# Window attention: queries and keys projected with their features on partitions, and rotated by a shuffle within 32 partitions

## The chip, the cores and the metric

The kernel runs on one core of one Trainium2 chip. Its time is the device time of one execution in microseconds (us); of three executions the median is given. A profile of one further execution shows what each engine did: TensorE (PE, and PEld for its weight loads), VectorE (DVE), ScalarE (ACT), GpSimd (POOL) and SyncE (SP, which here only issues transfers).

## The reference

An encoder of two layers works on 1024 tokens of 1024 features, all in float32. Layer 0 is the one that matters here: windowed attention with 16 query heads and 4 key and value heads of 64 features, rotary positions, a sink per head, and four further heads that attend to 256 memory tokens.

```python
u = rmsnorm(h, norm_g[layer, 0])
q, k, v, xq = jnp.split(u @ w_in, [ATT_Q_W, ATT_Q_W + ATT_KV_W, ATT_Q_W + 2 * ATT_KV_W], axis=-1)
q = rope(q.reshape(bsz, t, ATT_HEADS, ATT_HEAD_DIM), pos)
k = rope(k.reshape(bsz, t, ATT_KV_HEADS, ATT_HEAD_DIM), pos)
# rope: x1, x2 are the two halves of a head's 64 features
concatenate([x1 * cos - x2 * sin, x2 * cos + x1 * sin], axis=-1)
```

Each block of 128 queries then sees the keys of its own block and of both neighbours. An output projection, a convolutional feed-forward stage, a gated recurrence (layer 1) and a second feed-forward stage follow.

## The kernel before

Every float32 operand of a large product is split into a high part (a cast) and a low part (what the cast left over), and `mm3` (lines 79 to 82) adds three products: high by high, low by high, high by low. A weight unit is loaded by SP into a staging buffer, cast by ACT and subtracted by DVE or POOL (`wunit`, line 68). The normalised input, transposed so that features lie on partitions, stays in SBUF as `uh` and `ul`. It is scaled by the gain alone; the factor of each token (`rs0`) comes in later.

The start (`start`, line 1384) projects the memory for both layers while SP brings in the weights, the transposed input and the rows of x, of which ACT takes the sums of squares. Then `window` (line 242) goes through four groups `g`; each has four query heads and one key and value head. `proj(g)` computes a group's queries, keys and values, and `attend(g)` does its eight blocks. The program has them as proj(0), attend(0), proj(1), attend(1) and so on; `attend` also calls the memory heads (`cross_unit`, line 197), whose projections use the same PSUM banks.

In `proj`, `token(t)` (line 270) takes 128 tokens as the stationary side and a weight row of 384 columns (256 for queries, 64 keys, 64 values) as the moving one: 8 feature tiles of three matmuls into one PSUM bank `pj` (two buffers), tokens on partitions. DVE multiplies the first 320 columns by a cosine and, with the halves swapped, by a sine table (lines 285, 286), POOL adds (287, 288; the key columns twice), ACT and DVE write the value's two parts, scaled by `rs0` (290, 298). The tables of a token tile were scaled by `rs0` too (`rooted`, line 1375). After four tokens `turn` (line 300) transposes the results on PE, twelve transposes per half of the tokens, through a bank `ptq`, and ACT and DVE split them into `kh`, `kl` and the query tiles `qs`. In `attend` the scores are lines 362 and 363, the masked maximum is 365, the exponentials 372, the transposes of the probabilities 388 and the products with the values 391 and 392. POOL also issues the transfers that sum feed-forward weights in DRAM (`w2s`); one step of them follows each rope result (`sum_steps`).

No order is written by hand here. A scheduler puts the instructions of each engine into one fixed queue when the program is built: an engine takes them strictly in that order, and an instruction that waits holds back all behind it.

## Time and profile before

| what | value |
|---|---|
| median of three executions | 2655.19 us (2654.46 to 2659.24) |
| the profiled execution's own time | 2650.18 us |
| its span, from the first to the last instruction | 2648.4 us |
| TensorE busy | 2595.5 us, 98% of the span |
| DVE, ACT, POOL busy | 1768.2, 1395.1, 473.0 us |
| first projection matmul, last transpose of a rope result | 54.9 and 410.1 us |
| granted TensorE clock | 1.00 of full speed in every stretch read here |

A row of a group gives the source line, engine, operation, the tile written and those read, the shapes, the count, busy time and mean duration. A row of the timeline begins with start and duration in us; square brackets hold the idle time before it and what ended it. A row of waits gives microseconds in total, times, and the longest.

### The profile page before, as it was taken

To read this page: it belongs to the slowest core of one execution; us is meant where nothing else is said; L and a number is where in the kernel's file an instruction comes from. 1 tells how busy PE (TensorE), PEld (TensorE's weight loads), DVE (VectorE), ACT (ScalarE), POOL (GpSimd) and SP (SyncE) were. 2 spreads that over 40 slices of the span, in tenths; PEclk is the share of its full clock that TensorE was granted. 3 is DMA by queue.
4 is the path that set the end of the run, shared out by engine and by line. 5 is a ranking of instruction groups with operands and counts; after the bars stand their busy time and mean duration, and the time that the engine had idled before them with its cause. 6 is when DMAs were issued, how large, how long until landed. Compare 5 with 4: busy or idle time off the path is not lost. (4 is left out here: it accounts for less than half of the span.)

```text
span 2648.4 us, 38975 instructions
## 1 busy us (share of the span) xinstructions
PE 2595.5 (98%) x14372; PEld 2177.9 (82%) x14372; DVE 1768.2 (67%) x2948; ACT 1395.1 (53%) x2534; POOL 473.0 (18%) x520
## 2 busy tenths in 40 slices
PE   8999999999999999999999999999999999999998
PEld 7888887788888888887888888888887788888887
DVE  6788886578565655477668685876657665656447
ACT  6467676545444445455465564656434444444443
POOL 0321010211111100031224241322211111110013
PEclk9999999999999999999999999999999999999999
DMA  9782222367777756674235351113337778785666
GB/s 355 249 174 57 74 86 85 102 192 196 199 198 199 206 153 219 215 267 158 84 104 152 87 131 51 55 33 114 121 108 194 197 195 204 202 203 169 202 209 235
DMA packets 195727, 425.92 MB, mean 161 GB/s; under 512 B 20048, under 2 KB 56272, under 8 KB 189904
## 3 DMA queue, kind: packets, MB, share of 16 engines
q1 hardware_dynamic: 161552, 324.06, 37.9%
q0 software_dynamic: 24544, 90.19, 16.4%
q10 hardware_dynamic: 9440, 9.19, 1.0%
q8 instruction: 113, 1.85, 0.3%
q14 instruction: 78, 0.64, 0.1%
HBM read 330.04 MB, written 116.39 MB: 169 GB/s over the span
## 5 line engine op out<-in xcount | busy, mean ns | idle before, releaser
L86 DVE TENSOR_TENSOR wl<-st,wh 128x1024 fp32r<-128x1024 f32 (+1 forms) x238 | 262.4, 1109 | 316.6 <-ACT wh L85 286.1
L85 ACT CAST wh<-st 128x1024 fp32r<-128x1024 f32 (+1 forms) x238 | 222.2, 936 | 287.7 <-PE X L574 189.3
L80 PE MATMUL pj<-uh,wh 128*128 128x512 f32 x512 | 203.9, 399 | 2.8 <-DVE q L1129 1.3
L574 PE MATMUL X<-wh,wl 128*128 128x512 f32 x528 | 205.2, 390 | 0.0
L574 PE MATMUL X<-wl,wh 128*128 128x512 f32 x528 | 205.1, 390 | 0.0
L81 PE MATMUL pj<-ul,wh 128*128 128x512 f32 x512 | 202.6, 396 | 0.0
L82 PE MATMUL pj<-uh,wl 128*128 128x512 f32 x512 | 202.3, 395 | 0.0
L574 PE MATMUL X<-wh 128*128 128x512 f32 x528 | 198.9, 390 | 0.6 <-DVE c L1003 0.6
L80 PE MATMUL pj<-wh,uh 128*128 128x384 f32 (+1 forms) x512 | 189.1, 371 | 3.4 <-DVE xl L86 1.3
L82 PE MATMUL pj<-wh,ul 128*128 128x384 f32 (+1 forms) x512 | 187.2, 366 | 0.0
L81 PE MATMUL pj<-wl,uh 128*128 128x384 f32 (+1 forms) x512 | 187.1, 365 | 0.0
L574 PE MATMUL V<-uh,wh 128*128 128x512 f32 x336 | 130.9, 390 | 0.0
L574 PE MATMUL V<-ul,wh 128*128 128x512 f32 x336 | 130.9, 390 | 0.0
L574 PE MATMUL V<-uh,wl 128*128 128x512 f32 x336 | 130.9, 390 | 0.0
L76 DVE TENSOR_TENSOR wl<-st,wh 128x1024 fp32r<-128x1024 f32 (+1 forms) x91 | 112.1, 1236 | 24.7 <-ACT wh L75 22.7
L75 ACT CAST wh<-st 128x1024 fp32r<-128x1024 f32 (+1 forms) x97 | 97.7, 1014 | 39.5 <-PE pj L81 16.4
L574 PEld LDWEIGHTS X<-wh 128*128 128x128 f32 x528 | 99.2, 188 | 21.4 <-issue 1.0
L574 PEld LDWEIGHTS X<-wl,wh 128*128 128x128 f32 x528 | 99.2, 188 | 20.5
L574 PEld LDWEIGHTS X<-wh,wl 128*128 128x128 f32 x528 | 99.2, 188 | 20.5
L80 PEld LDWEIGHTS pj<-uh,wh 128*128 128x128 f32 x512 | 96.3, 188 | 22.0 <-DVE q L1129 1.8
L962 POOL TENSOR_TENSOR c<-c,g 128x512 f32<-128x512 f32 x24 | 43.8, 1843 | 389.3 <-PE X L574 319.4
L1225 POOL TENSOR_TENSOR E<-EP,q 128x256 f32<-128x256 f32 x64 | 61.4, 959 | 288.9 <-DVE EP L1218 272.7
(411 smaller groups left out, 7219.1 us busy)
## 6 DMA issues: line engine op xcount, KB each, us to landing
st<-hid SPq DMA_DIRECT2D x154, 256.0 KB, 3.2
st<-in_ffw_dram SPq DMA_DIRECT2D x108, 256.0 KB, 3.5
w2s<-in_ffw_dram POOLq DMA_DIRECT2D x24, 1024.0 KB, 8.4
st<-in_ffw_dram SPq DMA_DIRECT2D x46, 512.0 KB, 4.4
hid<-tt SPq DMA_DIRECT2D x88, 256.0 KB, 4.7
st<-w2s SPq DMA_DIRECT2D x88, 256.0 KB, 3.4
sx<-in_ffw_dram SPq DMA_DIRECT2D x84, 256.0 KB, 3.9
sy<-in_ffw_dram SPq DMA_DIRECT2D x42, 512.0 KB, 6.5
```

The costliest lines, as they stand in the source:

```text
L75: act.copy(h[:, :n], raw)
L76: (eng or dve).tensor_tensor(l[:, :n], raw, h[:, :n].bitcast(F32), op=ALU.subtract)
L80: pe.matmul(o, ah, bh, start=first, stop=False)
L81: pe.matmul(o, ah, bl, start=False, stop=False)
L82: return pe.matmul(o, al, bh, start=False, stop=last)
L85: act.copy(h, src)
L86: dve.tensor_tensor(l, src, h.bitcast(F32), op=ALU.subtract)
L574: last = pe.matmul(o, x, y, start=new, stop=e, skip_group_check=not first)
L962: pool.tensor_tensor(y[q][:, t, :], y[q][:, t, :], g3[:, c], op=ALU.mult)
L1225: pool.tensor_tensor(gl, pl_, ql, op=ALU.mult)
```

## The change

`proj` is written anew. The weight is now the stationary side: a unit of 128 output features (unit 0 has the 64 value and the 64 key features, units 1 and 2 two query heads each) by 512 tokens, so 24 matmuls of 512 columns fill one bank of `pj`, features on partitions. Per group there are three units by two halves, in three PSUM buffers; `ptq` is gone. A group's weights come in three transfers of 512 KB in place of four of 384 KB, and POOL splits one unit per group after the first in place of two.

The features of a head are laid out so that each partner stands 16 partitions away within 32. `rope` multiplies the bank by the cosine table on DVE, shuffles it within 32 partitions on DVE, and POOL multiplies by the sine table and adds. ACT casts and DVE subtracts, now out of SBUF, straight into `qs`, `kh` and `kl`; the keys go to both partition halves. Only the values are transposed, 64 features by 128 tokens, four per half. Their norm factor stands in the table `ck`, whose lower half is the factor alone and whose upper half is the scaled cosine.

The tables are now 128 by 1024 each (cosine, sine, `ck`). `scaled_tables(b)` scales one half of the tokens: diagonals of `rs0` from DVE, a product with ones on PE that copies the factors onto all partitions, and products on DVE. The tables are loaded in halves, the first by `angles` as the last step of the start and the second within `proj(0)`.

```diff
-QKV_POOL = (0, 2, 2, 2)
+QKV_POOL = (0, 1, 1, 1)
...
-        tags = {"pj": ("pj", 2, psq), "ps": ("ps", 2, psp), "pt": ("pt", 2, psp), "po": [lambda: psp.tile([P, 512], F32, tag="po", bufs=1, name="po")] * 2, "sm": 3}
+
+        tags = {"pj": ("pj", 3, psq), "ps": ("ps", 2, psp), "pt": ("pt", 2, psp), "po": [lambda: psp.tile([P, 512], F32, tag="po", bufs=1, name="po")] * 2, "sm": 3}
...
+        ones = tables.tile([P, P], F32, name="ones")
+        pool.memset(ones, 1.0)
+
+        def bank():
+            return psq.tile([P, 512], F32, tag="pj", bufs=3, name="pj")
+
+        def temp(tag):
+            return ea.tile([P, 512], F32, tag=tag, bufs=2, name=tag)
+
+        def scaled_tables(b):
+            hs = slice(b * 512, (b + 1) * 512)
+            rooted(slice(4 * b, 4 * b + 4))
+            dg = temp("t1").rearrange("p (a b) -> p a b", a=4)
+            sums = bank()
+            for t in range(4):
+                dve.tensor_scalar_mul(dg[:, t], ident, rs0[:, 4 * b + t:4 * b + t + 1])
+                pe.matmul(sums[:, t * P:(t + 1) * P], ones, dg[:, t], start=True, stop=True)
+            act.copy(ck[:64, hs], sums[:64])
+            for x in (cos, sin):
+                dve.tensor_tensor(x[:, hs], x[:, hs], sums, op=ALU.mult)
+            act.copy(ck[64:, hs], cos[64:, hs])
...
-            us = [wunit(A["wqkv"][g, u], 768, eng=pool if u < QKV_POOL[g] else None) for u in range(4)]
+            us = [wunit(A["wqkv"][g, u], eng=pool if u >= 3 - QKV_POOL[g] else None) for u in range(3)]
...
-            def token(t):
-                ps = psq.tile([P, 384], F32, tag="pj", bufs=2, name="pj")
...
-                    wh, wl = us[k // 2]
-                    c = slice((k % 2) * 384, (k % 2 + 1) * 384)
-                    m = slice(t * P, (t + 1) * P)
-                    mm3(ps, uh[:, k, m], ul[:, k, m], wh[:, c], wl[:, c], k == 0, k == KT - 1)
...
-                dve.tensor_tensor(c4(t1), c4(ps[:, :320]), cb, op=ALU.mult)
-                roped[0] = dve.tensor_tensor(c4(t2), c4(ps[:, :320])[:, :, ::-1, :], sb, op=ALU.mult)
-                pool.tensor_tensor(rq[:, :320], t1, t2, op=ALU.add)
-                done = pool.tensor_tensor(rq[:, 320:], t1[:, 256:], t2[:, 256:], op=ALU.add)
-                sum_steps[0].send(done)
...
-            def turn(b, rqs):
-                hs = slice(b * 512, (b + 1) * 512)
...
-                        pe.transpose(tp[:, tt, :], rqs[tt][:, w * P:(w + 1) * P], ident)
...
+            def project(u, b):
+                hs = slice(b * 512, (b + 1) * 512)
+                wh, wl = us[u]
+                ps = bank()
                 for k in range(KT):
+                    c = slice(k * P, (k + 1) * P)
+                    mm3(ps, wh[:, c], wl[:, c], uh[:, k, hs], ul[:, k, hs], k == 0, k == KT - 1)
+                return ps, hs
+
+            def rope(ps, hs, table, p=slice(0, P)):
+                a, x = temp("t1"), temp("qb")
+                dve.tensor_tensor(a, ps, table[:, hs], op=ALU.mult)
+                dve.stream_shuffle(x[p], ps[p], [i ^ 16 for i in range(32)])
+                pool.tensor_tensor(x[p], x[p], sin[p, hs], op=ALU.mult)
+                done = pool.tensor_tensor(x[p], a[p], x[p], op=ALU.add)
+                for _ in range(2 if sent[0] % 3 == 0 else 1):
+                    sum_steps[0].send(done)
+                sent[0] += 1
+                return a, x
+
+            def keys(b):
+                ps, hs = project(0, b)
+                if (g, b) == (0, 0):
+                    scaled_tables(0)
+                up_, dn = slice(64, 128), slice(0, 64)
+                a, x = rope(ps, hs, ck, up_)
+                vh, vl = [v[:, 4 * b:4 * b + 4, c * 64:c * 64 + 64] for c in range(2)]
+
+                def turn():
+                    tp = bank().rearrange("p (a b) -> p a b", a=4)[:, :, :64]
+                    for t in range(4):
+                        pe.transpose(tp[:, t], a[dn, t * P:(t + 1) * P], ident[dn, dn])
+                    cast = act.copy(vh, tp)
+                    dve.tensor_tensor(vl, tp, vh.bitcast(F32), op=ALU.subtract)
+                    return cast
+
+                for o in (up_, dn):
+                    act.copy(kh[o, hs], x[up_])
+                    dve.tensor_tensor(kl[o, hs], x[up_], kh[up_, hs].bitcast(F32), op=ALU.subtract)
+                return turn
+
+            def queries(w, b):
+                ps, hs = project(1 + w, b)
+                a = rope(ps, hs, cos)[1]
+                lo, hi = slice(0, 64), slice(64, 128)
+                q0, q1 = [ap_.tile([P, 512], F32R, tag="qs", bufs=8, name="qs") for _ in range(2)]
+                qs[2 * w][b], qs[2 * w + 1][b] = q0, q1
+                act.copy(q0[lo], a[lo])
+                dve.tensor_tensor(q0[hi], a[lo], q0[lo].bitcast(F32), op=ALU.subtract)
+                act.copy(q1[hi], a[hi])
+                dve.tensor_tensor(q1[lo], a[hi], q1[hi].bitcast(F32), op=ALU.subtract)
...
+            for b in range(2):
+                turn = keys(b)
+                queries(0, b)
+                cast = turn()
...
+                    for x, key in ((cos, "cos"), (sin, "sin")):
+                        nc.sync.dma_start(x[:, 512:], A[key][:, 512:])
+                queries(1, b)
+                if g == 0 and b == 0:
+                    scaled_tables(1)
+                    attend(0, kept, range(3))
...
-        wo0.begin(psq, ("pj", "pj", "ptq"), [y0[:, t, :] for t in range(NT)], {6: marks[3, 2], 7: marks[3, 2]})
+        wo0.begin(psq, ("pj",) * 3, [y0[:, t, :] for t in range(NT)], {6: marks[3, 2], 7: marks[3, 2]})
...
-            nc.sync.dma_start(cos, A["cos"])
-            nc.sync.dma_start(sin, A["sin"])
...
+        def angles():
+            for x, key in ((cos, "cos"), (sin, "sin")):
+                nc.sync.dma_start(x[:, :512], A[key][:, :512])
...
+        turned_in = np.array([0, 32, 16, 48])[:, None] + np.arange(16)
+        turned_in = turned_in.reshape(1, 64) + 64 * np.arange(5)[:, None]
+        w = np.concatenate([aw[:, 1280 + 64 * g:1280 + 64 * g + 64], aw[:, 1024 + 64 * g:1024 + 64 * g + 64],
+                            aw[:, 256 * g:256 * g + 256]], axis=1)
+        w[:, 64:] = w[:, 64 + turned_in.reshape(-1)]
+        qkv.append(units(w, P).reshape(3, P, 1024))
```

Three places in the queues. First DVE at the start of the stage, before the change, where `wl` are weight parts, `t` rope products and `pj` the projection's bank:

```order
L76 TENSOR_TENSOR wl<-st,wh 128x768 [waits DMAHW4_49,PE_49,Activation_49]
L76 TENSOR_TENSOR wl<-st,wh 128x768 [waits DMAHW6_49,PE_49,Activation_49]
L285 TENSOR_TENSOR t_704<-pj,cos 128x320 [waits PE_49]
L286 TENSOR_TENSOR t_705<-pj,sin 128x320
L1377 TENSOR_SCALAR xss<-xss 128x1
L298 SCALAR_TENSOR_TENSOR v<-pj,rs_86,v 128x64 [waits Activation_49]
L1380 TENSOR_SCALAR cos<-cos,rs_86 128x32 [waits Pool_49]
```

and the same place now, where `t_699` are the diagonals and `qb` is the shuffled copy:

```order
L1411 TENSOR_SCALAR xss<-xss 128x4 [waits Activation_49]
L1413 TENSOR_SCALAR xsc<-rs_86 128x4 [waits Pool_49]
L1414 TENSOR_SCALAR xsc<-rs_86 128x4
L76 TENSOR_TENSOR wl<-st,wh 128x1024 [waits DMAHW0_49,PE_49,Activation_49]
L281 TENSOR_SCALAR t_699<-ident,rs_86 128x128 x4
L451 TENSOR_SCALAR sk_642<-sk 128x16 [waits DMAHW5_49,DMAHW3_49,DMAHW1_49]
L285 TENSOR_TENSOR cos<-cos,pj 128x512 [waits Activation_49]
L285 TENSOR_TENSOR sin<-sin,pj 128x512
L307 TENSOR_TENSOR t_713<-pj,ck 128x512 [waits Activation_49]
L308 STREAM_SHUFFLE qb<-pj 64x512
L307 TENSOR_TENSOR t_750<-pj,cos 128x512 [waits DVE_49,PE_49]
L308 STREAM_SHUFFLE qb<-pj 128x512
```

The factors come for four token tiles at once; a weight split stands ahead of the diagonals, and four table and rope operations follow before the first shuffle is done.

Second, POOL's queue for the first projections, before (`rs` is the power, `rq` the rope sums):

```order
L1378 TENSOR_TENSOR rs_86<-xss,nhalf 128x1 [waits DVE_49]
L287 TENSOR_TENSOR rq<-t_704,t_705 128x320 [waits DVE_49,PE_49]
L288 TENSOR_TENSOR rq<-t_704,t_705 128x64
L143 DMA w2s_79<-in_ffw_dram 32x4x2048
L1378 TENSOR_TENSOR rs_86<-xss,nhalf 128x1 [waits DVE_49]
L287 TENSOR_TENSOR rq<-t_748,t_749 128x320 [waits DVE_49,PE_49]
L288 TENSOR_TENSOR rq<-t_748,t_749 128x64
L143 DMA w2s_79<-in_ffw_dram 32x4x2048
```

and now:

```order
L1412 TENSOR_TENSOR rs_86<-xss,nhalf 128x4 [waits DVE_49]
L309 TENSOR_TENSOR qb<-qb,sin 64x512 [waits DVE_49,PE_49,Pool_49]
L309 TENSOR_TENSOR qb<-qb,sin 128x512 [waits DVE_49,Pool_49]
L310 TENSOR_TENSOR qb<-t_713,qb 64x512 [waits Pool_49]
L143 DMA w2s_79<-in_ffw_dram 32x4x2048 x2
L310 TENSOR_TENSOR qb<-t_750,qb 128x512 [waits Pool_49]
L143 DMA w2s_79<-in_ffw_dram 32x3x2048
L1412 TENSOR_TENSOR rs_86<-xss,nhalf 128x4 [waits DVE_49]
L309 TENSOR_TENSOR qb<-qb,sin 128x512 [waits DVE_49]
L310 TENSOR_TENSOR qb<-t_806,qb 128x512 [waits Pool_49]
L143 DMA w2s_79<-in_ffw_dram 32x4x2048
```

A rope result was one pair of operations per token tile; now both products of the first two units stand ahead of the first sum, and the transfers ahead of the second.

Third, PE in the third group's attention with its memory head. `ps` are scores, `pt` transposes, `po` products with values. The longest piece without eight projection matmuls in a row was, before, one that begins so:

```order
L362 MATMUL ps<-kh,qs 128x384
L363 MATMUL ps<-kl,qs 128x384
L81 MATMUL po<-pl,kvh 128x512
L82 MATMUL po<-ph,kvl 128x512
L388 MATMUL pt<-ident,sm 128x128 x4
L362 MATMUL ps<-kh,qs 128x384
L363 MATMUL ps<-kl,qs 128x384
L362 MATMUL ps<-kh,qs 128x384
L363 MATMUL ps<-kl,qs 128x384
L362 MATMUL ps<-kh,qs 128x384
```

It holds 30 score matmuls up to the next such run; the next longest hold 26, 22 and 20. Now one of the two longest begins so, after three projection matmuls:

```order
L80 MATMUL pj<-uh,wh 128x512
L81 MATMUL pj<-ul,wh 128x512
L82 MATMUL pj<-uh,wl 128x512
L425 MATMUL po<-ph,v 128x512
L426 MATMUL po<-pl,v 128x512
L422 MATMUL pt<-ident,sm 128x128 x4
L232 MATMUL pt<-ident,xp 128x128 x4
L396 MATMUL ps<-kh,qs 128x256
L397 MATMUL ps<-kl,qs 128x256
L396 MATMUL ps<-kh,qs 128x256
L397 MATMUL ps<-kl,qs 128x256
L425 MATMUL po<-ph,v 128x512
```

The pieces now hold 48, 44 (this one), 28 and 28 score matmuls. Of DMA transfers, SP's queue now has both halves of the cosine and sine tables (256 KB each) in its first fifteen entries, next to the first piece of the transposed input, although the program has them later; before, it had a cosine table of 128 KB and a sine table of 256 KB there.

More of the change, by code (lines that the diff above doesn't have):

```diff
@@ L323, in proj @@
-            kept = (qs, kh, kl, v)
-            if g == 0:
-                rqs = [token(t) for t in range(5)]
-                turn(0, rqs[:4])
-                attend(0, kept, range(3))
-                turn(1, rqs[4:] + [token(t) for t in range(5, NT)])
-            else:
-                for b in range(2):
-                    turn(b, [token(t) for t in range(4 * b, 4 * b + 4)])
+                    c = slice(k * P, (k + 1) * P)
+                    mm3(ps, wh[:, c], wl[:, c], uh[:, k, hs], ul[:, k, hs], k == 0, k == KT - 1)
@@ new lines, in proj @@
+            kept = (qs, kh, kl, v)
+            for b in range(2):
[3 more added lines that the diff above has]
+                if g == 0 and b == 0:
+                    for t, tag in zip(range(5, NT), ("kh", "kl", "v")):
+                        row = ap_.tile([P, NT, P] if tag == "v" else [P, T], F32R, tag=tag, bufs=1, name="row").bitcast(F32)
+                        row = row.rearrange("p a b -> p (a b)") if tag == "v" else row
+                        nc.sync.dma_start(row, A["x"][t * P:(t + 1) * P, :])
+                        with tc.issue_after(cast.ins):
+                            act.activation(row, row, AF.Square, accum_out=xss[:, t:t + 1])
+                    for x, key in ((cos, "cos"), (sin, "sin")):
+                        nc.sync.dma_start(x[:, 512:], A[key][:, 512:])
+                queries(1, b)
+                if g == 0 and b == 0:
+                    scaled_tables(1)
+                    attend(0, kept, range(3))
@@ L332, in proj @@
             return kept
-        pairs, roped = {}, {}
+        pairs, sent = {}, [0]
         marks, moved = {}, []
@@ L359, in attend @@
                     for j in range(4):
-                        s = psp.tile([P, 384], F32, tag="ps", bufs=2, name="ps")
+                        s = score()
                         m = slice(nn * P, (nn + 1) * P)
```

59 lines of the change are left out of this document (10 added, 49 removed).

## The prediction

> **What bounds the kernel now.** I read the page first, then a table of stretches, then what TensorE (PE) waits for. Columns of the table: PE, weight loads, DVE, ACT, POOL busy, clock, DMA share, GB/s.
>
> ```profile
> PE 2595.5 (98%) x14372; PEld 2177.9 (82%) x14372; DVE 1768.2 (67%) x2948; ACT 1395.1 (53%) x2534; POOL 473.0 (18%) x520
> 0.00:60.00 60.00, 52.41 (x320) 47.50 (x321) 39.12 (x54) 42.29 (x59) 1.70 (x8) 1.00 0.99 371
> 60.00:100.00 40.00, 38.52 (x221) 36.73 (x219) 26.78 (x85) 15.09 (x36) 23.01 (x35) 1.00 0.87 293
> 100.00:300.00 200.00, 189.72 (x1092) 169.34 (x1093) 159.56 (x426) 135.40 (x348) 37.58 (x51) 1.00 0.51 122
> 300.00:420.00 120.00, 110.25 (x615) 94.04 (x614) 98.27 (x263) 87.27 (x217) 11.24 (x16) 1.00 0.29 85
> ```
>
> PE bounds the program. The change lies in the attention stage, 55 to about 500 us. Between 60 and 420 us PE is busy 338.5 of 360 us: 21.5 us are stalls. DVE is busy 285 us there, so it is a near second bound. The waits of PE in that stage:
>
> ```profile
> PE ps L362 <- DVE mx L365: 7.9, 13, 1.5
> PE po L392 <- DVE pl L86: 3.2, 5, 1.2
> PE pj L80 <- DVE v L298: 1.6, 2, 1.0
> PE ptq L310 <- POOL rq L288: 1.1, 1, 1.1
> PE ptq L310 <- POOL rq L287: 0.9, 3, 0.5
> ```
>
> Most stalls are attention steps that wait for DVE; projections are what PE does meanwhile. A saving on PE therefore counts fully only where projection work still fills the waits.
>
> **PE work.** The spacing of starts, not the duration, is the cost of a pipelined matmul.
>
> ```profile
> 64.91 0.34 PE L81 MATMUL pj<-wl,uh 128*128 128x384 f32 x1
> 68.72 0.34 PE L82 MATMUL pj<-wh,ul 128*128 128x384 f32 x1
> 68.90 0.49 PE L310 MATMUL ptq<-ident,rq 128*128 128x128 f32 x3
> 69.41 0.34 PE L81 MATMUL pj<-wl,uh 128*128 128x384 f32 x1
> 313.39 0.39 PE L81 MATMUL pj<-ul,wh 128*128 128x512 f32 x1
> 318.42 0.40 PE L82 MATMUL pj<-uh,wl 128*128 128x512 f32 x1
> 18.47 0.28 PE L82 MATMUL pb<-mh,wl 128*128 128x256 f32 x1
> 18.59 0.61 PE L1455 MATMUL pbc<-dg,ones 128*128 128x128 f32 x4
> 19.16 0.28 PE L81 MATMUL pb<-ml,wh 128*128 128x256 f32 x1
> ```
>
> The first two rows are matmuls 2 and 24 of one token tile: 3.81/22 = 0.173 us each. The two of 512 columns are also 22 starts apart: 5.03/22 = 0.229. Now 4 groups x 192 x 0.173 = 132.9 us; after, 4 x 144 x 0.229 = 131.9: **-1.0**. Three transposes sit between 68.72 and 69.41, where two ordinary steps take 0.35: 0.115 each. The 96 of them go: **-11.0**. The 32 new value transposes move 64 columns, between half (0.06) and all (0.115) of that; nearest in form, I take 0.09: **+2.9**. Two broadcasts of a diagonal take 0.69 less two 256-column steps (0.23) = 0.46 us; eight new ones: **+1.8**. Together PE does **7.3 us less**.
>
> **DVE, ACT and POOL.** Rows for the operations that go (duration min/median/max) and the nearest kept ones:
>
> ```profile
> L285 DVE TENSOR_TENSOR t<-pj,cos x32: 461/486/493, 62.9 to 393.8; 128x320 f32<-128x320 f32 x32
> L298 DVE SCALAR_TENSOR_TENSOR v<-pj,rs,v x32: 248/275/287, 64.2 to 395.6; 128x64 fp32r<-128x64 f32 x32
> L319 DVE TENSOR_TENSOR qs<-ptq,qs x16: 683/683/685, 80.0 to 413.7; 64x512 fp32r<-64x512 f32 x16
> L318 ACT CAST qs<-ptq x16: 568/580/584, 79.4 to 412.5; 64x512 fp32r<-64x512 f32 x16
> L287 POOL TENSOR_TENSOR rq<-t,t x32: 850/872/2281, 63.9 to 394.8; 128x320 f32<-128x320 f32 x32
> L288 POOL TENSOR_TENSOR rq<-t,t x32: 311/320/434, 64.7 to 395.7; 128x64 f32<-128x64 f32 x32
> L962 POOL TENSOR_TENSOR c<-c,g 128x512 f32<-128x512 f32 x24 | 43.8, 1843 | 389.3 <-PE X L574 319.4
> ```
>
> The trace has no shuffle. Bounds: 0.49 us (320 elements, from PSUM) and 1.22 (the 1024-element subtraction below); at 512 elements I take 0.69, that of L319. DVE loses 32 x (0.49 + 0.48 + 0.28) + 40 x 0.69 = 67.6 us and gains 24 x 0.69 products, 24 x 0.69 shuffles, 48 x 0.69 subtractions and 8 x 0.42 for values, 69.6 us; weight splits and table scaling come out within 2 us. At 1.22 the shuffles add 13. ACT keeps its load (72 casts at 0.31 to 0.59 us become 60). POOL: 0.87 and 0.32 for 320 and 64 elements make 1.28 at 512 by the straight line, 1.84 by L962; I take 1.28. Its 64 rope operations (38 us) become 48 (61 us, at most 88). That is idle time of POOL, but its two operations now stand between shuffle and ACT's cast, and whatever is queued on ACT behind that cast waits too.
>
> [...]
>
> **The start of the stage.** SP now issues four table pieces of 256 KB ahead of seven of the eight pieces of the transposed input, where two of 384 KB in all went: 640 KB more at 371 GB/s with the DMA engines 99% busy, up to 1.8 us later. Behind them wait ACT's casts and then PE. ACT has some slack, so I take **+1.0** (0 to 1.8). Then the chain that makes the tables:
>
> ```profile
> 54.86 0.33 PE L80 MATMUL pj<-wh,uh 128*128 128x384 f32 x1
> 59.10 0.19 ACT L1440 ACTIVATION_READ_ACCUMULATOR x<-x 128x1 f32 x1
> 47.03 1.05 ACT L75 CAST wh<-st 128x1024 fp32r<-128x1024 f32 x1
> L1378 POOL TENSOR_TENSOR rs<-xss,nhalf x8: 543/578/1060, 48.1 to 91.0; 128x1 f32<-128x1 f32 x8
> L76 DVE TENSOR_TENSOR wl<-st,wh x91: 950/1222/1765, 12.0 to 2008.5; 128x1024 fp32r<-128x1024 f32 x81, 128x768 fp32r<-128x768 f32 x10
> ```
>
> The first unit ends at 54.86 + 24 x 0.229 = 60.4. The first broadcast behind it needs the fourth row's sum (about 59.2 still), power (0.58), a weight split queued ahead on DVE (1.22), small steps and a diagonal (0.3 to 0.8): 61.4 to 61.9. Everything on PE queues behind it: **+1.3** (1.0 to 1.5). The value transposes wait for ACT's copy (0.58), two table products, the key product and the shuffle (4 x 0.69) after the last broadcast at about 66.1, so until 69.5; PE's remaining 8 matmuls end at 67.9: **+1.2** (0.5 to 1.6). The first scores wait for POOL: from 69.5 three operations of 1.28, two DMA issues (0.6 each), a fourth operation, ACT 0.58, DVE 0.69 = 77.1; PE has finished the second query unit at 75.4: **+1.7** (0 if the POOL steps are shorter, 4 at 1.84). The stall of 1.0 at L298 goes. Start together **+4.2**.
>
> **The steady part.** The other waits on L298 and ptq go: 1.6 + 1.1 + 0.9 less the 1.0 counted = **-2.6**. Against that stand two costs. First, filler. The longest stretches of PE order without eight projection matmuls in a row hold 30, 26, 22 and 20 score matmuls before, and 48, 44, 28 and 28 after, 50 more. What such a stretch costs, and the one that follows with projection work:
>
> ```profile
> 299.40:313.00 13.60, 11.34 (x61) 7.80 (x59) 12.59 (x40) 11.78 (x32) 0.00 (x0) 1.00 0.12 40
> 313.00:327.00 14.00, 13.62 (x75) 11.93 (x76) 11.02 (x28) 11.74 (x32) 0.00 (x0) 1.00 0.21 57
> ```
>
> The first is the stretch of 30: 2.3 us idle, DVE 93% busy. 50/30 x 2.3 = 3.8 us, less what fuller stretches elsewhere recover (0 to 3.8): **+2.5**. Second, DVE and POOL hold each other up:
>
> ```profile
> 115.91 0.86 POOL L287 TENSOR_TENSOR rq<-t,t 128x320 f32<-128x320 f32 x1 [15.89 <-DVE t L286]
> 116.28 0.52 DVE L377 TENSOR_TENSOR su<-su,es 128x4 f32<-128x4 f32 x1
> L377 DVE TENSOR_TENSOR su<-su,es x32: 143/161/599, 98.1 to 479.1; 128x4 f32<-128x4 f32 x32
> ```
>
> A sum of 4 columns takes 0.52 instead of 0.16 us and ends when POOL does (116.8). The change puts both inputs of the 48 subtractions into SBUF and lengthens POOL's operations. POOL is busy about 69 of 360 us with two kinds of work of 1.28: a chance near 0.2 of meeting one with half of it (0.64) left, 0.13 us for each of 48, 6 us, and some 0.07 more for about 160 others, 11 us: 0 to 17 us on DVE. I let **+2.0** reach PE.
>
> Sum: -7.3 + 1.0 + 4.2 - 2.6 + 2.5 + 2.0 = -0.2. I round it to **no change that can be measured** and state -1, because -7.3 is counted from rows and the stalls are only bounded. The profiled execution took 2650.2 (span 2648.4, 1.8 around it), 5.0 under the median 2655.2; against the median -1 is **2654**.
>
> **The rivals.** (1) Faster: the stalls at the start are hidden and the later ones only replace others. For it: from 60 to 100 us DVE is busy 26.8 of 40 us, so its part of the chain can come early. Then -7.3 - 2.6 + 2 = -8, **2647**; with nothing added -10. Chance 0.36. (2) Slower: DVE is held off by POOL. [...] As a mechanism here: of the 17 us at most 12 reach PE in stretches where DVE is 93% busy, in place of the 2.0: +10, **2665**. It decides from about 0.1 us per subtraction. Against it: the casts before the subtractions follow POOL's last step, so a pair rarely meets. Chance 0.27. (3) The lengthened PE stretches alone use up the saving: that is the forecast, 0.37.
>
> **How the numbers follow.** About 0.2% (5 us) is what a measurement of this kernel can tell from no change. No change 0.37, faster 0.36, slower 0.27. The forecast's own range is 2650 to 2660. The whole range goes from -7.3 - 2.6 - 4 of further stalls (2641) to +12 (2667), with the shuffle at its upper bound only partly inside.
>
> **What would show it.** Right: PE busy about 7 us lower, shuffles at 0.6 to 0.8 us, PE waits of 1 to 2 us at the first broadcast, transposes and scores between 60 and 78 us, and more idle PE in the two long stretches. Wrong: no stall there and fewer idle microseconds from 100 to 420 (rival 1), or subtractions and small sums whose mean has risen by over 0.1 us (rival 2); a shuffle of over 1 us would break the DVE sum.

## The result and the profile after

The changed kernel takes **2682.75 us** (median of 4 runs, 2676.09 to 2686.53) beside 2655.46 us before: ratio **1.0097**, 95% interval 1.0075 to 1.0120. It is slower by 27 us, beyond the upper end of the range (2667). The profiled execution has a span of 2681.7 us against 2648.4: 33.3 us to explain.

The page's line of the engines, and the table of stretches (columns: PE, weight loads, DVE, ACT, POOL busy, granted clock, DMA share, GB/s), of the kernel after:

```profile
PE 2606.5 (97%) x14132; PEld 2158.1 (80%) x14132; DVE 1796.6 (67%) x2917; ACT 1401.0 (52%) x2518; POOL 492.9 (18%) x496
0.00:60.00 60.00, 50.01 (x294) 44.86 (x295) 38.12 (x48) 38.84 (x52) 1.29 (x8) 0.97 0.97 366
60.00:100.00 40.00, 32.09 (x141) 25.50 (x140) 24.20 (x51) 17.90 (x34) 14.57 (x13) 0.91 0.66 220
100.00:300.00 200.00, 186.74 (x913) 153.17 (x912) 167.03 (x388) 126.30 (x304) 64.07 (x53) 0.96 0.54 140
300.00:420.00 120.00, 108.94 (x554) 88.62 (x554) 96.05 (x234) 78.84 (x193) 18.51 (x12) 0.97 0.19 53
```

Two things the sum did not have, or had far smaller. PE has 240 matmuls less and yet is busy 11.0 us *longer*, and the granted clock, 1.00 in every stretch before, is below it in all of these. And DVE is busy 28.4 us longer (1796.6 against 1768.2) with 31 instructions fewer. PE's idle time (span less busy) rose from 52.9 to 75.2 us.

The clock in detail. PE's timeline of the kernel after, at the first scores (start, duration, instruction, idle time before it and its releaser), with some steps left out:

```profile
80.24 0.39 PE L81 MATMUL pj<-ul,wh 128*128 128x512 f32 x1
80.46 0.39 PE L82 MATMUL pj<-uh,wl 128*128 128x512 f32 x1
84.58 0.58 PE L396 MATMUL ps<-kh,qs 128*128 128x256 f32 x1 [3.73 <-DVE qs L344]
...
89.12 0.63 PE L82 MATMUL pj<-uh,wl 128*128 128x512 f32 x1
89.55 0.63 PE L80 MATMUL pj<-uh,wh 128*128 128x512 f32 x1
...
91.47 0.40 PE L82 MATMUL pj<-uh,wl 128*128 128x512 f32 x1
91.70 0.39 PE L80 MATMUL pj<-uh,wh 128*128 128x512 f32 x1
```

The same matmul starts every 0.22 us ahead of the wait, every 0.43 behind it, every 0.23 from 91.5 us on. The wait cost its 3.7 us and then some more at half clock. Stretches of 10 us in which it happened again:

```profile
80.00:90.00 10.00, 4.76 (x15) 3.31 (x14) 9.80 (x19) 3.01 (x5) 7.35 (x7) 0.72 0.92 297
240.00:250.00 10.00, 7.16 (x28) 5.04 (x26) 9.37 (x25) 9.06 (x24) 0.00 (x0) 0.74 0.19 58
290.00:300.00 10.00, 6.86 (x21) 5.30 (x20) 6.84 (x19) 6.81 (x22) 0.00 (x0) 0.66 0.00 0
```

PE is busy 5 to 7 of 10 us in them. I took stretches of 4 us up to 700 us and added up idle time (length less busy) and half clock (PE busy times one minus the clock). Before: 32.4 us idle, 0 at half clock. After: 52.1 idle, 16.4 at half clock. That is 36.1 us more; PE's own work, busy less half clock, fell from 2595.5 to 2590.1. Together 30.7 of the 33.3 us. By place, idle and half clock: 4.0 more up to 60 us, 8.9 more from 60 to 100, 9.9 from 100 to 300, 4.1 from 300 to 420, 9.1 from 420 to 560.

The profiled execution of the kernel before flatters it: with 2650.18 us and a mean granted clock of 1.000 it is the fastest on record. The 51 executions of that kernel measured beside the experiments took 2650.93 to 2661.96 us, with a clock of 0.995 to 0.999. So most of the step from 27 to 33.3 us, and probably some of the 16.4, belong to this one execution and not to the change.

### The profile page after: what moved, and what is told of

It reads as the page before. It is cut to its first block, busy times and chain, and to the rows that moved or that the text cites. A ratio compares the mean times of both kernels' runs of the same rounds, so it can differ in the third digit from the quotient of the medians.

```text
span 2681.7 us, 38334 instructions
## 1 busy us (share of the span) xinstructions
PE 2606.5 (97%) x14132; PEld 2158.1 (80%) x14132; DVE 1796.6 (67%) x2917; ACT 1401.0 (52%) x2518; POOL 492.9 (18%) x496
## 5 line engine op out<-in xcount | busy, mean ns | idle before, releaser
L86 DVE TENSOR_TENSOR wl<-st,wh 128x1024 fp32r<-128x1024 f32 (+1 forms) x238 | 262.3, 1108 | 319.0 <-ACT wh L85 284.2
L85 ACT CAST wh<-st 128x1024 fp32r<-128x1024 f32 (+1 forms) x238 | 222.4, 936 | 288.9 <-PE X L608 190.5
L80 PE MATMUL pj<-uh,wh 128*128 128x512 f32 x704 | 283.3, 403 | 9.2 <-DVE qb L308 4.4
L81 PE MATMUL pj<-ul,wh 128*128 128x512 f32 x704 | 280.2, 398 | 0.0
L82 PE MATMUL pj<-uh,wl 128*128 128x512 f32 x704 | 279.1, 396 | 0.0
L82 PEld LDWEIGHTS pj<-uh,wl 128*128 128x128 f32 x704 | 133.8, 190 | 26.7
L81 PEld LDWEIGHTS pj<-ul,wh 128*128 128x128 f32 x704 | 134.4, 191 | 25.8 <-DVE ul L86 0.4
L76 DVE TENSOR_TENSOR wl<-st,wh 128x1024 fp32r<-128x1024 f32 x90 | 115.7, 1291 | 24.9 <-ACT wh L75 23.2
L608 PEld LDWEIGHTS X<-wl,wh 128*128 128x128 f32 x528 | 99.1, 188 | 21.3 <-DVE wl L86 0.7
L75 ACT CAST wh<-st 128x1024 fp32r<-128x1024 f32 x93 | 97.3, 1048 | 34.6 <-PE pj L81 17.6
L80 PE MATMUL pj<-wh,uh 128*128 128x512 f32 x256 | 101.6, 398 | 1.2 <-DVE gs L1149 1.2
```

The source lines that it names most:

```text
L75: act.copy(h[:, :n], raw)
L76: (eng or dve).tensor_tensor(l[:, :n], raw, h[:, :n].bitcast(F32), op=ALU.subtract)
L80: pe.matmul(o, ah, bh, start=first, stop=False)
L81: pe.matmul(o, ah, bl, start=False, stop=False)
L82: return pe.matmul(o, al, bh, start=False, stop=last)
L85: act.copy(h, src)
```

## Experiments

All ratios are to the kernel before, each run with it on the same chip. "Idle" and "half clock" are the sums just described. The first column names the runs as the text below does.

```
run                                         us       ratio (95%)               idle  half clock
(the changed kernel)                        2682.75  1.0097 (1.0075 to 1.0120)  52.1  16.4
tables late                                 2681.71  1.0094 (1.0077 to 1.0111)  46.9  15.9
first scores later                          2683.61  1.0104 (1.0084 to 1.0124)  52.5  16.0
two projection, three score banks           2682.34  1.0097 (1.0081 to 1.0112)  50.0  16.7
first wait filled                           2679.31  1.0091 (1.0075 to 1.0108)  46.9  13.4
POOL's rotation on 64 columns               2665.29  1.0038 (1.0023 to 1.0053)  41.5  11.2
  and its load put back beside the chain    2673.78  1.0074 (1.0057 to 1.0091)  44.5  14.4
POOL's rotation on DVE, repeated            2676.99  1.0075 (1.0057 to 1.0093)  46.2  16.2
sine product on DVE, sum on POOL            2678.65  1.0092 (1.0076 to 1.0109)  49.2  13.0
three normalisations on ACT                 2673.99  1.0073 (1.0058 to 1.0088)  48.1  12.1
  the same in the kernel before             2654.77  1.0002 (0.9992 to 1.0011)  31.7   5.7
64 columns, three on ACT, tables late       2666.52  1.0046 (1.0031 to 1.0061)  42.1  14.4
  and units behind the scores               2658.98  1.0017 (1.0007 to 1.0026)  37.7  10.4
units behind the scores alone               2681.30  1.0094 (1.0079 to 1.0109)  54.6  16.3
```

### The waits that the trace names: three edits that gain nothing

My first theory was that the named waits, and the clock that they cost, are the loss. Three edits took one each.

**Tables late.** The scheduler had put all four table loads ahead of weights and input; this puts them behind the rows of x.

```diff
+            with tc.issue_after(last[0].ins):      # the load of row 4 of x
                 for x, key in ((cos, "cos"), (sin, "sin")):
                     nc.sync.dma_start(x[:, :512], A[key][:, :512])
+                    with tc.issue_after(late.ins): # the load of row 7; then the second halves
```

> The changed kernel with the four table loads (4 x 256 KB, that the scheduler had put ahead of the second weight loads of the memory keys) behind the fifth row of x and behind the last row. Theory: the first projection matmul, at 59.7 us in the changed kernel and 54.9 before, comes at 55 to 56 us, the stretch 35 to 40 us keeps its clock, and the time falls by 4 to 5 us, to about 2678. Rival (the tables were hidden, the head is late for another reason): 2682 to 2683.

The head came back (the second row is the same group in the changed kernel, which starts at 59.7), and the time did not:

```profile
L80 PE MATMUL pj<-uh,wh x20: 389/391/628, 54.8 to 74.9; 128*128 128x512 f32 x20
```

```profile
L80 PE MATMUL pj<-uh,wh x16: 389/389/475, 59.7 to 72.5; 128*128 128x512 f32 x16
```

Most of the 4.9 us went again in a longer wait for the first broadcast (2.39 instead of 1.42 us) and in 5.2 instead of 2.5 us at half clock from 60 to 100 us, and the wait of 3.7 us at the scores stayed: the first scores start 2.4 us earlier (82.21 for 84.58), those after the next projections 0.9 (93.79 for 94.66). The tables do make the head late, but the chain behind it decides when the attention starts.

**First scores later.** `project(0, 1)` is traced ahead of the first `attend`, and its scores ordered behind its last matmul.

```diff
                     scaled_tables(1)
-                    attend(0, kept, range(3))
+                    begun = project(0, 1)
+                    with tc.issue_after(ended[0].ins):
+                        attend(0, kept, range(3))
```

> The changed kernel with the first scores of group 0 traced and ordered behind the next projection (24 more matmuls, 5.5 us). Clock theory: the wait of 3.7 us at 84.6 us goes, and with it the half clock from 84 to 92 us (another 3.3 us): 7 us less, about 2676. Rival (a wait costs its length): 3.7 us less at most, 2679; and if the wait only moves to the broadcast of the second half's factors, which now stands ahead: no change, 2682 to 2683.

The wait moved, as the last sentence allowed, and grew. PE's timeline of this run:

```profile
88.90 0.80 PE L282 MATMUL pj<-t,ones 128*128 128x128 f32 x2 [6.81 <-DVE t L281]
```

**Banks.** Scores get the third bank, projections keep two.

```diff
         def score():
+            turn_[0] += 1
+            if turn_[0] % 3 == 0:
+                return psq.tile([P, 512], F32, tag="ps3", bufs=1, name="ps")[:, :384]
             return psp.tile([P, 384], F32, tag="ps", bufs=2, name="ps")
...
-            return psq.tile([P, 512], F32, tag="pj", bufs=3, name="pj")
+            return psq.tile([P, 512], F32, tag="pj", bufs=2, name="pj")
```

> The changed kernel with two PSUM banks for projections instead of three, and the bank given to the scores (three instead of two). Theory that the scores' banks set the waits in the stretches without projections: PE's wait for the mask-max (6.7 us in 7) falls under 3 us, and since these waits lower the clock at 240, 280, 330 and 440 us, up to 10 us of half clock go too: 2668 to 2676. Rival (the chain DVE, POOL, ACT holds a projection's bank so long that three are needed): the waits of pj for the rotation (4.4 us) grow by 5 us or more and the time is 2683 to 2695.

The rival came true for the waits, but not for the time. The waits of PE from 60 to 420 us, of this run (wait, us in total, times, longest):

```profile
PE pj L80 <- DVE qb L312: 10.0, 9, 4.0
PE ps L400 <- DVE mx L403: 6.6, 6, 1.8
```

and of the changed kernel:

```profile
PE ps L396 <- DVE mx L399: 5.3, 4, 2.3
PE pj L80 <- DVE qb L308: 4.4, 5, 2.1
```

Waits that are taken away at one place and come back at another point to a rate that lies elsewhere.

### What lowers the clock

The waits' price at half clock was measured by itself. `burst(x, n)` is n matmuls of 128x512, `wait(ps, k)` k dependent copies on DVE, `turned` transposes.

```diff
+    ps = burst(x, 80)
+    for k in (1, 2, 3, 4, 5, 6, 8):
+        x = wait(ps, k)
+        ps = burst(x, 80)
+    for n, k in ((2, 1), (4, 1), (6, 1), (8, 1), (3, 2), (6, 2), (9, 2), (12, 2)):
+        for _ in range(10):
+            x = wait(ps, k)
+            ps = burst(x, n)
+        x = wait(ps, 1)
+        ps = burst(x, 80)
+    x = wait(ps, 1)
+    ps = turned(x, 100)
+    x = wait(ps, 1)
+    ps = burst(x, 80)
```

> Leaves the whole computation out: bursts of 80 matmuls (128x512) are parted by chains of 1 to 8 dependent VectorE copies that PE waits for, then come eight series of ten short bursts (2 to 12 matmuls) with one or two such copies between, then 100 transposes. [...] Idle-length form: no wait of 1 or 2 us lowers the clock, however many follow each other. Share form: the series with 2 matmuls per wait (PE at work well under half of the time) run at half clock, those with 8 or 12 at full. Rival: the spacing of 0.43 seen in the changed kernel has another cause (operands, ports), and here every spacing is 0.22.

PE's timeline: each row is a burst, with the wait ahead of it in brackets. 80 matmuls take 18.43 us at full clock.

```profile
107.88 20.04 PE L38 MATMUL ps<-x,idr 128*128 128x512 f32 x80 [2.63 <-DVE x L45]
131.00 18.45 PE L38 MATMUL ps<-x,idr 128*128 128x512 f32 x80 [3.09 <-DVE x L45]
153.47 20.01 PE L38 MATMUL ps<-x,idr 128*128 128x512 f32 x80 [4.01 <-DVE x L45]
175.78 0.73 PE L38 MATMUL ps<-x,idr 128*128 128x512 f32 x2 [0.78 <-DVE x L43]
179.13 1.22 PE L38 MATMUL ps<-x,idr 128*128 128x512 f32 x2 [0.78 <-DVE x L43]
193.18 20.67 PE L38 MATMUL ps<-x,idr 128*128 128x512 f32 x80 [0.78 <-DVE x L43]
231.18 2.07 PE L38 MATMUL ps<-x,idr 128*128 128x512 f32 x4 [0.79 <-DVE x L43]
280.64 1.64 PE L38 MATMUL ps<-x,idr 128*128 128x512 f32 x6 [0.79 <-DVE x L43]
564.49 11.14 PE L51 MATMUL pt<-ident,x 128*128 128x128 f32 x100 [0.78 <-DVE x L43]
576.41 18.43 PE L38 MATMUL ps<-x,idr 128*128 128x512 f32 x80 [0.78 <-DVE x L43]
```

In these series the share form held and the idle-length form did not. Waits of 0.78 us were enough: with 2 matmuls between them (0.45 us of work in 1.52, 30%) the clock halved at the third (granted 1.00 from 172 to 176 us, 0.50 from 178 to 192), with 4 (0.91 in 1.98, 46%) at the eighth (1.00 from 214 to 228 us, 0.50 from 230 to 236), with 6 (1.36 in 2.45, 56%) in none of ten; near the border a series of 6 with waits of 1.25 us (47%) kept it too. A single wait of 2.63 us halved it (the burst behind it took 20.04 us), one of 3.09 did not (18.45), one of 4.01 did (20.01): its length alone did not decide. Each series ran once. After the series of 2 the full burst took 20.67 us, 2.2 more than 18.43, which at half clock is some 4 us until it was back.

In the kernel itself: **first wait filled** with matmuls of no use.

```diff
+                        if (g, n, j) == (0, 0, 0):
+                            with tc.issue_after(ended[0].ins):
+                                for _ in range(30):
+                                    pe.matmul(s[:, :w], uh[:, 0, :P], uh[:, 0, :w], start=True, stop=True)
```

> The changed kernel with 30 matmuls of 256 columns (0.113 us each, 3.4 us) ahead of the first score, in the bank that the score then overwrites; the score waits for its query as before, at about 84.6 us. Clock theory: the granted clock, 0.59 to 0.50 from 84 to 90 us in the changed kernel, stays at 1.00, and the projections behind the wait start 0.23 us apart instead of 0.43: the 9 that start from 88.1 to 91.5 us take about 2.1 instead of 3.4 us, and the point that the changed kernel reaches at 94.66 us (the next scores) comes 2 to 2.5 us earlier. Rival (the wait is not what lowers the clock): spacing 0.43 and the point unchanged. The whole time may hide 2 us in the scatter: 2678 to 2684.

Stretches of 2 us, of the changed kernel:

```profile
84.00:86.00 2.00, 0.79 (x2) 0.50 (x2) 1.97 (x2) 0.00 (x0) 1.92 (x2) 0.59 0.96 319
86.00:88.00 2.00, 1.12 (x3) 0.83 (x4) 1.97 (x7) 0.62 (x1) 1.91 (x2) 0.50 1.01 315
88.00:90.00 2.00, 2.00 (x7) 1.61 (x7) 1.94 (x8) 0.61 (x1) 0.00 (x0) 0.50 0.93 258
```

and of the run with the wait filled:

```profile
84.00:86.00 2.00, 1.91 (x16) 1.71 (x15) 1.54 (x2) 1.02 (x2) 2.00 (x3) 1.00 1.03 377
86.00:88.00 2.00, 0.50 (x2) 0.30 (x2) 1.97 (x4) 0.00 (x0) 1.92 (x2) 1.00 0.98 332
88.00:90.00 2.00, 1.40 (x4) 1.26 (x5) 1.97 (x9) 1.23 (x2) 0.83 (x2) 0.53 1.01 352
```

The filled wait keeps the clock. But two short waits follow (1.26 and 0.92 us, two scores between them), and these halve it at 88 us: the half clock begins 4 us later and ends at the same 91 us. So the expected 2 us became 1.0 (2.5 to 1.5 us at half clock from 60 to 100 us), and the whole time shows nothing.

### GpSimd

**POOL's rotation on 64 columns**, and the same with its load put back beside the chain:

```diff
-                pool.tensor_tensor(x[p], x[p], sin[p, hs], op=ALU.mult)
-                done = pool.tensor_tensor(x[p], a[p], x[p], op=ALU.add)
+                n = slice(0, 64)
+                pool.tensor_tensor(x[p, n], x[p, n], sin[p, n], op=ALU.mult)
+                done = pool.tensor_tensor(x[p, n], a[p, n], x[p, n], op=ALU.add)
+                # second run only, twice, behind `done`:
+                pool.tensor_tensor(a[p], sin[p, hs], sin[p, hs], op=ALU.mult)
```

> The changed kernel with GpSimd's two operations of every rotation on 64 of the 512 columns; the rest of the rotation's product and sum is left out, so that its time is that of a rotation almost without GpSimd. Theory POOL (its two operations of 1.29 us lengthen the chain behind every projection by 2.4 us, and VectorE stands still behind them: one VectorE operation on 4 elements takes up to 1.27 us, the sums of the SBUF operations are 15 us above those of before): both go, VectorE falls from 1796 to about 1780 us busy, PE idle and half clock (52 and 16 us up to 700 us) fall to under 35 and 5, and the time comes to 2652 to 2662. Rival order (the projection units of 512 columns run ahead of the scores, and the attention is left without filler whatever the chain costs): 2673 or more.

> As the run with GpSimd's operations on 64 columns (the same part is left out), but two products of 512 columns that nobody waits for are put back on GpSimd behind them: the chain stays short, the load on GpSimd is the changed kernel's. If GpSimd costs through the stand of VectorE: the time is near the changed kernel's, 2672 to 2682. If it costs through the length of the chain: near the run without it, within 4 us.

17 of the 27 us go with GpSimd's columns, between the two branches. (The rest of the rotation's product and sum is left out, in this run and in those below that build on it.) The page's line of the run on 64 columns:

```profile
PE 2600.1 (98%) x14132; PEld 2153.8 (81%) x14132; DVE 1770.3 (67%) x2917; ACT 1400.9 (53%) x2518; POOL 444.9 (17%) x496
```

DVE has the same 2917 instructions and is busy 26.3 us less: that long it had stood behind GpSimd, counted as busy. One example of the changed kernel, POOL's timeline and then DVE's:

```profile
178.93 1.28 POOL L309 TENSOR_TENSOR qb<-qb,sin 128x512 f32<-128x512 f32 x1 [3.10 <-DVE su L411]
180.28 2.76 POOL L76 TENSOR_TENSOR wl<-st,wh 128x1024 fp32r<-128x1024 f32 x1
182.99 1.42 POOL L310 TENSOR_TENSOR qb<-t,qb 128x512 f32<-128x512 f32 x1
```

```profile
179.16 1.60 DVE L346 TENSOR_TENSOR qs<-qb,qs 64x512 fp32r<-64x512 f32 x1 [0.35 <-ACT qs L345]
181.26 3.36 DVE L417 TENSOR_SCALAR sm<-sm,rd 128x384 f32<-128x384 f32 x2
```

The subtraction takes 1.60 instead of 0.69 us and ends some 0.5 us behind POOL's product (178.93 + 1.28 = 180.21); two normalisations that take 0.8 us together last 3.36, through a weight split on POOL. With the load put back (second run) 16 of the 26 us return to DVE (1786.3) and the ratio goes from 1.0038 to 1.0074, outside the other's interval: GpSimd's load costs, though nobody waits for its result. The two causes are not quite parted: the operations that were put back stand in POOL's queue ahead of the next rotation, and ACT's casts wait 17.6 us for the rotation's sums from 60 to 420 us (10.9 without them, 21.3 in the changed kernel). What the length of the chain adds on top (1.0074 to 1.0097) is inside the intervals; it stays open.

**On DVE instead.** The first form of this run says nothing: its stand-in on POOL waited for nothing, so the weight sums of the feed-forward began at the start, the first projection came at 151.6 us, and it took 2771 us (1.0432, 1.0417 to 1.0448).

```diff
+                dve.tensor_tensor(x[p], x[p], sin[p, hs], op=ALU.mult)
+                dve.tensor_tensor(x[p], a[p], x[p], op=ALU.add)
-                done = pool.memset(tick, 0.0)                  # first form
+                done = pool.tensor_copy(tick[p], x[p, :1])     # repeated
```

> The changed kernel with the two GpSimd operations of every rotation on VectorE: 48 operations of about 0.69 us more on it (33 us), 15 us of standing still less, the chain 1.2 us shorter. If VectorE's load sets the time of this stage: slower, 2690 to 2700. If the standing still and the chain do: 2670 to 2678.

> The changed kernel with the two GpSimd operations of every rotation on VectorE, and a copy of one column on GpSimd behind them, so that the loads that follow GpSimd's sums keep their time. VectorE: 48 operations of about 0.69 us more (33 us), 15 us of standing still less, the chain 1.2 us shorter. If GpSimd's hold of VectorE is the main cost: below the changed kernel, 2670 to 2680. If VectorE's load counts the same wherever it comes from (9 us of time for 15 us in the run with three normalisations on ScalarE): 18 us net give +10, less 4 for the chain: 2686 to 2692.

Repeated, it takes 2676.99, as the first branch said. The page's line:

```profile
PE 2608.5 (97%) x14132; PEld 2160.6 (81%) x14132; DVE 1798.1 (67%) x2965; ACT 1402.4 (52%) x2518; POOL 430.1 (16%) x472
```

48 more operations on DVE, 33 us by their durations, and DVE is busy 1.5 us longer: nearly all that GpSimd took over it took back by standing in the way. Half of the move, **the sine product on DVE and the sum on POOL**, was expected slower and changes nothing (1.0092):

```diff
+                dve.tensor_tensor(x[p], ps[p], sin[p, hs], op=ALU.mult)   # sine signs turned round
+                dve.stream_shuffle(x[p], x[p], [i ^ 16 for i in range(32)])
-                pool.tensor_tensor(x[p], x[p], sin[p, hs], op=ALU.mult)
```

> The changed kernel with the rotation computed the other way round: VectorE multiplies the PSUM bank by the sine table, shuffles the product, and only the sum is left to GpSimd. VectorE has 24 operations of 0.69 us more (16.6 us), GpSimd half of its 61 us less, the chain 0.6 us shorter. By VectorE's load alone: +17 less half of the 15 us of standing still, so 5 to 9 us slower, 2687 to 2691. By the earlier runs' prices (load and lock on GpSimd 8.5 us, its chain 8.5 us, halved, against 16.6 us at the price of 0.6 us per us of VectorE's load that the run with three normalisations on ScalarE gave): +1 to +3, 2682 to 2686.

### Is DVE the pace?

**Three of four normalisations on ACT** instead of two, in both kernels:

```diff
-                        if j < 2:
+                        if j < 3:
                             act.activation(sm[:, j, :w], ..., AF.Copy, scale=st["rd"][:, j:j + 1])
```

> The changed kernel with three of four (instead of two of four) normalisations of the exponentials on ScalarE: 32 operations of 0.475 us (15 us) less on VectorE, 32 of 0.6 us (19 us) more on ScalarE. If VectorE's load sets the pace of the attention (80 to 87 per cent busy from 100 to 420 us): 2668 to 2675. If latency and order set it: 2680 to 2685.

> The kernel before with three of four normalisations on ScalarE. If VectorE's pace in the attention binds there too, about 8 us less, 2647; if the attention of the kernel before has slack on VectorE (77 to 83 per cent busy from 100 to 300 us, PE never idle for long): no change within 3 us.

9 us by the medians in the changed kernel (the intervals, 1.0058 to 1.0088 and 1.0075 to 1.0120, overlap); nothing at all before, where PE and DVE had more room. That run of the kernel before has 5.7 us at half clock, most of it from 300 to 330 us: it is not immune to the clock either.

### All together, and the order of the units

> The changed kernel with three edits of the earlier runs together: GpSimd's two operations on 64 of 512 columns (the rest of the rotation's product and sum is left out), three of four normalisations on ScalarE, table loads behind the rows of x. If the loss is VectorE's pace in the attention (GpSimd's lock, its own operations) plus the head, the gains of the single runs (17, 8 and 1 us of 2682) add up: 2653 to 2658, at the time of the kernel before. If the coarser projection units cost something by themselves, the gains overlap and it stays at 2660 or above.

The gains did not add: 2666.5, the same as with GpSimd's columns alone. Both relieve DVE, and one is enough. So 11 us had another cause. A candidate was in sight: in the kernel before, the first scores of group 1 start at 182.07 us, with projection units spread between its blocks; in the changed kernel they start at 208.46, behind 81 projection matmuls with no score between (two units of the memory heads, one and part of a second of group 2), and later scores are left without. **Units behind the scores** orders PE so:

```diff
+GATE = (1, 2, 3, 5, 6, 7)
             def project(u, b):
+                with tc.issue_after(scored[g - 1, GATE[3 * b + u]].ins) if g else nullcontext():
```

> The changed kernel with the six projection units of groups 1 to 3 ordered on PE behind the scores of blocks 1, 2, 3, 5, 6 and 7 of the group ahead, one unit per block; in the changed kernel four to eight units of the next group stand ahead of block 8. Theory order: idle and half clock between 200 and 420 us (21 and 10 us in the changed kernel, 13 and 0 before) fall to 15 and 2, and the time to 2664 to 2670. Rival (the pace of VectorE and ScalarE sets the attention, whatever stands beside it): 2679 to 2685, with the idle time moved.

> The same order of units together with GpSimd's operations on 64 of 512 columns (the rest of the rotation's product and sum is left out), three of four normalisations on ScalarE and the late table loads: the run of these three without the order gave 2666.5. Theory order: the remaining 11 us go, 2652 to 2657. Rival: 2663 to 2668.

Alone it does nothing: 1.0094, idle and half clock only moved (from 100 to 300 us they go from 20.1 to 18.6, from 420 to 560 from 11.6 to 14.6). With DVE relieved it takes 1.0046 to 1.0017, intervals apart. Stretches of that last run:

```profile
60.00:100.00 40.00, 33.53 (x146) 26.73 (x145) 23.31 (x62) 17.51 (x34) 9.19 (x16) 0.91 0.73 260
100.00:300.00 200.00, 193.27 (x993) 159.65 (x992) 154.25 (x398) 143.09 (x345) 33.68 (x49) 1.00 0.52 134
300.00:420.00 120.00, 109.82 (x556) 89.46 (x555) 95.72 (x258) 88.22 (x221) 7.66 (x12) 0.96 0.26 73
```

From 100 to 300 us the clock is at 1.00 again and PE is busier than before the change (193.3 against 189.7). What is left against the kernel before is 4 us. Idle time and half clock are still 15.6 us above it, of which PE's lighter work makes up some 10; the largest part lies from 60 to 100 us, where the chain from the rows' sums to the first scores makes PE wait (9.5 us idle and at half clock against 1.5).

Whole kernels with these edits did not beat the kernel before:

> The changed kernel with the rotation's product on VectorE as in the run beside it, three of four normalisations on ScalarE, and the table loads behind the rows of x. By the single prices: VectorE's load as in the changed kernel, half of GpSimd's cost gone (8 us), the head 1 to 4 us: 2669 to 2673; faster than the kernel before only if the gains do more than add.

> A whole kernel: the order of units, the rotation's product on VectorE, three of four normalisations on ScalarE, the late table loads; without the order 2672.0. Theory order: 2655 to 2663. Rival: 2669 to 2674. Faster than the kernel before by either only if the clock holds at 1.00 throughout (16 us of half clock in the run without the order).

> A whole kernel without GpSimd in the rotation: both operations on VectorE, all four normalisations on ScalarE (30 us less on VectorE, 38 more on ScalarE), the order of units and the late tables. VectorE's load is then near that of the run without GpSimd's operations and two units of order (2659.0): 2660 to 2668 if ScalarE has room (52 to 53 per cent busy over the whole, 63 to 66 in this stage), 2675 or more if ScalarE becomes the pace.

They measured 2672.0 (1.0068), 2671.8 (1.0060) and 2686.5 (1.0111). The first two differ by the order of the units alone, and it is worth nothing there, although three normalisations are on ACT and DVE is as busy from 100 to 420 us as in the kernel before (258.0 and 257.6 us, 257.8 before). So the 7.5 us of the order are seen only where GpSimd's columns are left out, and what holds the whole kernels back is not DVE's busy time alone; it stays open. In the last run PE waits longest for ACT's `ph` (11.7 us from 100 to 520 us, 5.2 in the changed kernel), which fits ACT becoming the pace with all four normalisations on it, but does not show it: ACT is busy 71% from 100 to 420 us there and 72% in the run of 2658.98.

## Why the prediction was wrong

**PE's work, -7.3: right in size, useless.** Without the half clock PE has 5.4 us less to do. Matmuls start 0.22 to 0.23 us apart as priced, and the four value transposes of a half 0.08 (0.46 less one of 0.22, over three; 0.09 was taken). It did not reach the time, since PE waits for DVE more than it gained.

**DVE, equal loads: right for the rotation's own operations, wrong for DVE.** The unit prices held (duration min/median/max; below them the group of the small sums, with its busy time and mean in ns):

```profile
L308 DVE STREAM_SHUFFLE qb<-pj x24: 720/737/755, 74.3 to 393.9; 128x512 f32<-128x512 f32 x16, 64x512 f32<-64x512 f32 x8
L309 POOL TENSOR_TENSOR qb<-qb,sin x24: 1279/1296/2297, 75.2 to 394.8; 128x512 f32<-128x512 f32 x16, 64x512 f32<-64x512 f32 x8
L411 DVE TENSOR_TENSOR su<-su,es x32: 144/161/1267, 101.0 to 507.0; 128x4 f32<-128x4 f32 x32
```

```profile
L411 DVE TENSOR_TENSOR su<-su,es 128x4 f32<-128x4 f32 x32 | 9.1, 283 | 17.4 <-ACT sm L406 12.9 <-ACT es L404 4.6
```

Shuffle 0.74 for 0.69, POOL 1.29 for 1.28; undisturbed, the rotation's operations take 70.4 us where those that went took 67.2, 3.2 us more for the 2.0 predicted. DVE's line rose by 28.4 us.

**The step that failed is "DVE and POOL hold each other up", 0 to 17 us on DVE, of which +2.0 reaches PE.** What failed is above all the +2.0: taking GpSimd's columns away saves 17 us of time, and putting its load back beside the chain costs 8.5 of them again. On DVE the columns are worth 26.3 us, but not all of that is new. Two groups of normalisations show it, of the memory heads (L227) and of the window (L383, later L417 and L418). Before:

```profile
L227 DVE TENSOR_SCALAR xp<-xp,rd 128x256 f32<-128x256 f32 x64 | 23.7, 434 | 0.7
L383 DVE TENSOR_SCALAR sm<-sm,rd 128x384 f32<-128x384 f32 (+1 forms) x64 | 23.9, 416 | 0.5
```

In the changed kernel:

```profile
L227 DVE TENSOR_SCALAR xp<-xp,rd 128x256 f32<-128x256 f32 x64 | 23.8, 434 | 0.7
L417 DVE TENSOR_SCALAR sm<-sm,rd 128x384 f32<-128x384 f32 (+1 forms) x64 | 30.4, 516 | 0.6
```

With GpSimd on 64 columns:

```profile
L227 DVE TENSOR_SCALAR xp<-xp,rd 128x256 f32<-128x256 f32 x64 | 18.3, 350 | 0.8
L418 DVE TENSOR_SCALAR sm<-sm,rd 128x384 f32<-128x384 f32 (+1 forms) x64 | 25.0, 431 | 0.4
```

L227 takes 5.4 us more than with 64 columns, and took as much before the change; with the maxima (L368, 9.1 us for 5.8) the kernel before stood some 9 us already. Compared row by row, about 17 us are new, the upper end of the bound. (So the 17 us of time may hold a gain that the kernel before could have had too; no run took GpSimd's work away there.) They fell elsewhere than expected: 3.0 us on the 48 subtractions (35.9 us, 33.0 with 64 columns; 6 were estimated), and some 14 on the others (11 estimated), 6.5 of them on the window's normalisations. The bound came from a chance of meeting half an operation. The trace shows whole operations of POOL being waited for (a sum of 4 columns up to 1.27 us, the length of a POOL operation), and POOL's weight splits of 2.76 us in the same role.

Rival 2 was this mechanism, with the right sign and the price 2665; it held that PE would feel 12 us at most, an estimate. In the changed kernel DVE stood on operations with two SBUF inputs (a subtraction of 1.60 us for 0.69) and also on the normalisations, which read one SBUF tensor and a column of factors: 0.516 us in the mean, 0.431 with GpSimd on 64 columns.

**The second part of the failure has no term in the sum: a wait was priced at its length.** The clock at half costs 16.4 us more than in the profiled execution before, which lost none. It also suggests why filler counts for more than its own idle time: in that execution PE is never under 7.7 of 10 us busy from 80 to 500 us and keeps its clock; after, the same kind of waits come bunched, 4.8 to 7.2 of 10 us, and halve it.

**Longer stretches without projections, +2.5: not settled.** With GpSimd's columns left out the order of the units is worth 7.5 us; in the changed kernel and in the whole kernels it is worth nothing. That a pace other than PE's decides there fits, but no run shows it alone.

**The start, +4.2: right by place, too small.** The broadcast waits 1.42 us (1.3 predicted), the transposes 0.94 (1.2), the first scores 3.73 (1.7, upper bound 4). The tables make the first projection 4.8 us later, not 1.0 (0 to 1.8): weights came late three times (waits of 1.19, 1.08 and 0.76 us from 23 to 36 us), and the clock averaged 0.66 from 35 to 40 us. Yet putting the tables right moved no time. The prediction's sum counts the tables' +1.0 twice, alone and within the +4.2; it should read -1.2 in place of -0.2, which changes nothing in the forecast. The waits on L298 and `ptq`, -2.6, went as predicted, and others came.

Of the signs named, shuffles, the three waits and the idle stretches were there. Rival 2's sign was half there: the small sums' mean rose from 0.183 us before to 0.283, just the 0.1 us from which it was to decide, but that of the subtractions only by 0.06, from 0.69 to 0.75.

## What to carry to other kernels

When work is handed to GpSimd beside a VectorE that is 80% busy, take GpSimd's whole busy time as an estimated upper bound of what it adds to VectorE's load (here 26 of the rotation's 70 us were felt): here the profile counted the standing as busy (1.27 us for a sum that takes 0.16), and moving the work back made DVE only 1.5 us busier. In a kernel that TensorE bounds, look for 10-us stretches in which its busy time, multiplied by the granted clock, is about half or less (3.43, 5.30 and 4.53 us in the three shown): here such stretches cost their idle time and then part of the 16.4 us at half clock, and in the bursts waits of 0.78 us were enough. And when one wait is taken away and the time stays, stop chasing waits and ask which engine's rate they share; here that answered for up to 17 of 27 us.

## What the runs showed of the hardware

In the series of bursts the clock went with the share of work and not only with the length of a wait: waits of 0.78 us with 46% of work between them halved it after about 15 us, and with 56% they did not in ten rounds; a single wait of 2.63 us halved it, one of 3.09 did not. Transposes kept it up: 100 of them in 11.14 us left the next burst at full clock (18.43 us). GpSimd's operation on 512 columns took 1.29 us for 64 partitions as for 128.

Not tried: keeping the clock up through all the short waits, and POOL's weight splits on DVE.
